# The first expert set's loop for leftover blocks, moved from behind its last unit to ahead of it

## The chip, the cores and the metric

The kernel runs on one core of a Trainium2 chip. It is one launch; the metric is its device time in microseconds. The core's engines each work through an instruction list of their own: TensorE (PE, with its weight loads as PEld), VectorE (DVE), ScalarE (ACT), GpSimd (POOL) and SyncE (SP), which here mainly issues the DMA transfers from HBM.

## The reference

Two transformer blocks follow one another on 512 tokens of width 1024, in fp32. Each ends with a mixture of experts. In the first, a token goes to 2 of 32 experts:

```python
hid = jax.nn.silu(a) * u * gates[:, sl, None].astype(hf.dtype)
out = out + jnp.einsum('nef,efd->nd', hid, w_d[sl]).astype(jnp.float32)
```

`a` and `u` are a token's products with an expert's gate and up matrix (1024 to 256), `w_d` leads back from 256 to 1024. The second block begins with `h = rms_norm(x, g_mix_norm) * (1.0 + scale_m) + shift_m` on the sum of all this, and projects `h` with `w_in` (`proj = h @ w_in`). Its own mixture has 64 experts, 6 for a token.

## The kernel before

The stages stand in the order of the program: `phase_a` (attention of the first block), `phase_b` (its experts), `phase_c` (mixer of the second block), `phase_d` (its experts). Here it is the end of `phase_b` and the start of `phase_c`.

**Units.** The tokens of an expert fill slots of 32, 64 or 128 rows; a unit is 128 rows from two or three experts, which were ranked by their number of tokens. The first set has 13 units (0 to 12), the second 33; unit 12 has three experts (64, 32 and 32 rows). For a unit SP loads three matrices of 1 MB for each expert: `wg`, `wu`, `wd` (`load`, line 802), so nine for unit 12, up to three units ahead (`fetch`). `main` makes on PE the product `g` with `wg` and `u` with `wu` (line 973), on ACT and DVE `hid` from both (lines 975 and 979), on PE the transposed `hT` (984), then the product `y` with `wd` (997), which ACT and DVE split into a high and a low part, `yh` and `yl`. The scatter (`scatter`, lines 1051 and 1052) multiplies these with the 0/1 matrix `st` on PE into banks `sc`, and DVE adds each to the residual `xres`. The scatter of a unit is made within the next unit's `main`, between `u` and `y`, most of it ahead of `hT`; that of unit 12 comes at the end of `run`. PE's and DVE's order inside `main` is that of the code; all else is ordered by a scheduler.

**The loop for leftover blocks.** Tokens that find no slot go through `spill`: a loop (line 1144) with a count that is known only at run time. Each turn loads one expert and treats 128 rows of it. Where a loop begins, all engines meet, SP also with the transfers of its queue; the loop's body is left out if the count is zero. In `phase_b` it stands behind everything else:

```python
moe.run()
early[1](moe.gathered.ins)
...
early[2](junk)
moe.spill(lambda: early[2](junk))
```

Here `early[1]` has POOL make the row `gs` of the next norm.

**What comes next.** `early[2]` is `stats` (line 1472): for each of four blocks of 128 tokens ACT sums the squares (into a waste tile `junk`), and `rsqrt` (lines 87 to 97) makes the factor `rs`. `phase_c` then makes `h` from `xres`, `rs` and `gs` on DVE (line 1511, eight halves), PE transposes it (`xt`, 1514), ACT and DVE split it into `xh` and `xl` (1518, 1519), and the projection `pr` (lines 108 to 110) multiplies both with the high and low parts `wh` and `wl` of `w_in` (`weights`: load 130, ACT 136, POOL 137). Two pieces of `w_in` have room at a time. The load of `mw` (line 1398) is for later sums.

Of the kernel before, what the change touches and what calls it, by code (L numbers as in the profile page):

```python
# [7 lines left out]
F32 = mybir.dt.float32  # L8
F32R = mybir.dt.float32r
# [11 lines left out]
KD = 8  # L21
# [724 lines left out]
class Moe:  # L746
# [182 lines left out]
        c = FIRST[self.E] + u  # L929
        self.xs[u] = self.slots(self.sel.pop(u), self.k.cols[:, c:c + 1], None, self.xg[u % 2])  # L930

    def turn(self, xg):
        k, nc, m = self.k, self.k.nc, self.m
        xT = m.tile([128, KD, 128], F32, tag="xT", name="xT", bufs=1)
        for h in range(2):
            b = k.bank("xT")
            for j in range(4):
                nc.tensor.transpose(b[:, j * 128:(j + 1) * 128], xg[:, 4 * h + j::8], k.ident)  # L938
            nc.scalar.activation(xT[:, 4 * h:4 * h + 4], b.rearrange("p (k s) -> p k s", k=4), AF.Copy)
        return xT  # L940
# [64 lines left out]
            self.k.nc.vector.tensor_mul(y, b, self.scale[:, h * 512:(h + 1) * 512])  # L1005
        return y

    def parts(self, out):

        k, m = self.k, self.m  # L1010

        def put(h, b):
            yh = m.tile([128, 512], F32R, tag="yh", name="yh", bufs=2)
            yl = m.tile([128, 512], F32R, tag="yl", name="yl", bufs=2)
            out.append((yh, yl))
            k.split(yh, yl, self.scaled(h, b, b))
        return put
# [34 lines left out]
                nc.vector.tensor_add(self.acc[:, t, hs], self.acc[:, t, hs], b)  # L1052
                yield

    def run(self):
        n = len(self.units)
        for u in range(2):
            self.pick(u)
        self.prep(0)
        with self.k.tc.issue_after(self.indexed.ins):  # L1060
            self.prep(1)
        if self.E == 32:
            self.fetch(3, after=self.gathered.ins, free=NF)
        self.take(0)
        self.pick(2)
        self.prep(2)
        self.table()
        self.pick(3)
        for u in range(n):
            self.fetch(u + FA)  # L1070
            with self.k.tc.manual_schedule(engines={self.k.nc.tensor.engine, self.k.nc.vector.engine}):
                self.main(u)
        for _ in self.scatter(*self.sofar.pop()):
            pass
# [64 lines left out]
    def spill(self, then=None):  # L1139

        k, nc, tc, m, E = self.k, self.k.nc, self.k.tc, self.m, self.E
        tbl = self.tbl
        n = nc.values_load(self.nb[0:1, 0:1], min_val=0, max_val=NB - 1)
        with tc.For_i(0, n, 1) as i:
            row = m.tile([128, 4], F32, name="row")
            nc.sync.dma_start(row, tbl[bass.ds(i, 1), :].to_broadcast([128, 4]))
            ei = m.tile([1, 1], I32, name="ei")
            nc.vector.tensor_copy(ei, row[:1, 3:4])
            ev = nc.sync.value_load(ei[0:1, 0:1], min_val=0, max_val=E - 1)
            ws = [(128, self.load([ev])[0])]  # L1150
            sel = m.tile([128, 128], F32R, name="selx")
            nc.vector.tensor_scalar(sel, row[:, 2:3].to_broadcast([128, 128]), k.cols[:, 0:1], None, op0=ALU.is_equal)
            xg = self.xg[0]
            st = self.slots(sel, k.cols[:, 2:3], row[:, 0:1], xg)
            gc = m.tile([128, 1], F32, name="gcx")
            jk = m.tile([128, E], F32, name="jkx")
            nc.vector.scalar_tensor_tensor(jk, k.tok[:, :E], row[:, 1:2], xg[1], op0=ALU.is_equal, op1=ALU.mult,
                                           accum_out=gc)
            y = []
            self.ffn(self.turn(xg[0]), ws, gc, self.parts(y))  # L1160
            for _ in self.scatter(st, y):
                pass
            if then is not None:
                then()
# [48 lines left out]
def top1(k, pool, v, n, name):  # L1213

    nc = k.nc
    shp = list(v.shape)
    mx = pool.tile(shp[:-1], F32, name=name + "m")
    oh = pool.tile(shp, F32, name=name + "o")
    nc.vector.tensor_reduce(mx, v, axis=AX.X, op=ALU.max)
    bc = lambda a: a.unsqueeze(len(shp) - 1).to_broadcast(shp)  # L1220
    nc.vector.tensor_tensor(oh, v, bc(mx), op=ALU.is_equal)
    rv = k.rev[:, None, 64 - n:].to_broadcast(shp)
    nc.vector.tensor_mul(oh, oh, rv)
    fm = pool.tile(shp[:-1], F32, name=name + "f")
    nc.vector.tensor_reduce(fm, oh, axis=AX.X, op=ALU.max)
    nc.vector.tensor_tensor(oh, rv, bc(fm), op=ALU.is_equal)
    return oh, mx


def phase_b(k, early):  # L1230
# [3 lines left out]
    def order():  # L1234
        while True:
            yield from OB
# [4 lines left out]
    moe = Moe(k, 32, I["w_exp_gate"][0], I["w_exp_up"][0], I["w_exp_down"][0], None, ctx, UNITS1, RB, order(), expert=expert)  # L1241
# [11 lines left out]
    gc = p.tile([128, KD], F32, name="gc")  # L1253
# [7 lines left out]
    def turn(t):  # L1261
        for q in range(2):
            b = k.bank("xt")
            for j in range(4):
                c = (4 * q + j) * 128
                nc.tensor.transpose(b[:, j * 128:(j + 1) * 128], k.xres[:, t, c:c + 128], k.ident)
            nc.scalar.activation(xTs[:, t % 2, 4 * q:4 * q + 4], b.rearrange("p (k s) -> p k s", k=4), AF.Copy)

    def logits(t):
        for kk in range(KD):  # L1270
            nc.tensor.matmul(lbs[0][:, t * 36:(t + 1) * 36], lhsT=xTs[:, t % 2, kk], rhs=wr[:, kk], start=kk == 0,
                             stop=kk == KD - 1)
# [23 lines left out]
    def rest():  # L1296
        moe.rooms()
        moe.work()
        early[0](k.wloads[-1])
        moe.fetch(2, 0, spread=[None] * NW + [written[i] for i in WS])  # L1300
        turn(NT - 1)
        logits(NT - 2)
        logits(NT - 1)
        moe.acc, lb = k.xres, lbs[0]
        v = Carve(moe, (("yh", 2), ("yl", 2)))
        L = v.tile([128, NT, 36], F32, name="L")
        for t in range(NT):
            nc.vector.scalar_tensor_tensor(L[:, t], lb[:, t * 36:(t + 1) * 36], rss[t], br, op0=ALU.mult, op1=ALU.add)
        go, gm = top1(k, v, L[:, :, :4], 4, "g")
        es = v.tile([128, NT, 4, 8], F32, name="es")  # L1310
        nc.vector.tensor_mul(es, L[:, :, 4:].rearrange("p t (g e) -> p t g e", g=4),
                             go[:, :, :, None].to_broadcast([128, NT, 4, 8]))
        sel = v.tile([128, NT, 8], F32, name="selv")
        nc.vector.tensor_reduce(sel, es.rearrange("p t g e -> p t e g"), axis=AX.X, op=ALU.add)
        o1, m1 = top1(k, v, sel, 8, "e")
        nc.vector.scalar_tensor_tensor(sel, o1, NEG, sel, op0=ALU.mult, op1=ALU.add)
        o2, m2 = top1(k, v, sel, 8, "f")
        on = v.tile([128, NT, 8], F32, name="on")
        nc.vector.tensor_add(on, o1, o2)

        def spread_(eng, dst, src):
            eng.tensor_mul(dst.rearrange("p t (g e) -> p t g e", g=4), src[:, :, None, :].to_broadcast([128, NT, 4, 8]),
                           go[:, :, :, None].to_broadcast([128, NT, 4, 8]))
        A = p.tile([128, NT, 32], BF, name="A")
        spread_(nc.vector, A, on)

        po = nc.gpsimd
        eg = v.tile([128, NT, 4], F32, name="eg")
        po.tensor_sub(eg, L[:, :, :4], gm[:, :, None].to_broadcast([128, NT, 4]))
        nc.scalar.activation(eg, eg, AF.Exp)  # L1330
        po.tensor_sub(m2, m2, m1)
        nc.scalar.activation(m2, m2, AF.Exp)
        gs = v.tile([128, NT], F32, name="gs")
        with tc.high_priority(-HP):
            nc.vector.tensor_reduce(gs, eg, axis=AX.X, op=ALU.add)
            nc.vector.scalar_tensor_tensor(gs, m2, 1.0, gs, op0=ALU.add, op1=ALU.mult)
            nc.vector.reciprocal(gs, gs)
        po.tensor_mul(m2, m2, gs)
        b8 = lambda a: a[:, :, None].to_broadcast([128, NT, 8])
        po.tensor_mul(o1, o1, b8(gs))  # L1340
        po.tensor_mul(o2, o2, b8(m2))
        po.tensor_add(o1, o1, o2)
        G = v.tile([128, NT, 32], F32, name="G")
        spread_(po, G, o1)
        moe.positions(A, v, perm)
        moe.ranked(G, v, p)
        moe.run()
        early[1](moe.gathered.ins)
        junk = moe.slot([128, 2, D], F32, "junk")
        k.root(moe.silu)  # L1350
        early[2](junk)
        moe.spill(lambda: early[2](junk))
        ctx.close()
        k.wr_ctx.close()
    return head, rest
# [696 lines left out]
```

## Time and profile before

| | us |
|---|---|
| three runs: lowest, median, highest | 1668.68, 1671.65, 1672.71 |
| the profiled execution, its own time | 1676.92 |
| its span | 1675.2 |
| PE busy in the span | 1550.9 (93%) |
| unit 12's `g` starts | 597.05 |
| last scatter of the first set ends on PE | 621.20 |
| first loads of `phase_c` leave SP | 627.66 |

The span is cut from the first to the last instruction on the chip; all starts below are from its begin. A timeline row gives start, length, engine, line, operation and in brackets the engine's idle time ahead of it and what ended it. Rows of a queue (SPq) are issues. A row with a count is merged from so many instructions.

### The profile page before, as it was taken

Reading aid. Unit: us, or ns where it says so; the run is one execution under the profiler, and the core shown is the slowest. Engines: PE = TensorE matmul, PEld = TensorE weight load, DVE = VectorE, ACT = ScalarE, POOL = GpSimd, SP = SyncE. Lnnn points to the kernel's source line nnn. Section 1 sums busy time; section 2 is a strip of 40 time slices with the busy share of each in tenths; the row PEclk is TensorE's granted clock in tenths of the full one; section 3 lists DMA queues with packets and bytes.
Section 4 is the critical chain, followed back from the end, with each engine's and each line's share of the span. In section 5 each row is a group of like instructions: output and inputs, shape, how many; then the busy total and the mean of one; then the engine's idle time right before and its main releaser. Section 6 shows DMA issues by size and latency. Waiting matters only on the chain.

```text
span 1675.2 us, 28638 instructions
## 1 busy us (share of the span) xinstructions
PE 1550.9 (93%) x10917; PEld 1060.7 (63%) x10917; DVE 970.1 (58%) x2219; ACT 542.3 (32%) x1090; POOL 347.4 (21%) x287
## 2 busy tenths in 40 slices
PE   5899999978998877899999998999999999999996
PEld 5665557765565546675667777865666666666663
DVE  3598536853564348547455534555665665656656
ACT  4534676331211125555553322301211211112112
POOL 2323551012111103330104441131111101111000
PEclk9999999987999998999999999899999999999998
DMA  5443336468999953233006837748899999999961
GB/s 187 147 162 114 107 82 233 132 214 321 418 416 417 419 239 105 72 104 90 26 5 203 255 104 276 285 168 366 366 411 386 396 412 415 418 414 422 419 259 64
DMA packets 104207, 420.78 MB, mean 251 GB/s; under 512 B 23444, under 2 KB 30074, under 8 KB 66692
## 3 DMA queue, kind: packets, MB, share of 16 engines
q1 hardware_dynamic: 82880, 389.25, 60.5%
q0 software_dynamic: 9968, 19.04, 3.1%
q10 hardware_dynamic: 11220, 10.63, 2.0%
q8 instruction: 87, 1.43, 0.3%
q14 instruction: 52, 0.43, 0.1%
HBM read 419.99 MB, written 9.21 MB: 256 GB/s over the span
## 4 chain that ended last, share of the span: by engine, by line
PE 46%; DVE 5%; DMA 4%; POOL 1%; ACT 1%; issue 1%; SPq 0%; DVEq 0%; ACTq 0%; POOLq 0%
PE g L973 8%; PE u L973 8%; PE sc L1051 7%; PE y L997 7%; PE qk L1671 2%; DMA mw<-in_w_mod_dram 2%; PE ob L1699 2%; PE xT L938 2%; PE pt L110 1%; PE pt L109 1%; PE pt L108 1%; PE pt L1691 1%; DVE macc L1400 1%; POOL wl L137 1%; DMA gmr<-in_g_ffn_norm_dram 1%
## 5 line engine op out<-in xcount | busy, mean ns | idle before, releaser
L137 POOL TENSOR_TENSOR wl<-w,wh 128x1024 fp32r<-128x1024 f32 (+4 forms) x72 | 166.7, 2316 | 366.4 <-ACT wh L136 343.9
L1052 DVE TENSOR_TENSOR xres<-xres,sc 128x512 f32<-128x512 f32 x368 | 224.5, 683 | 4.2 <-PE sc L1051 1.0
L973 PE MATMUL u<-wu,xT 128*32 128x256 f32 (+2 forms) x2240 | 180.4, 388 | 12.3 <-DMA wu<-in_w_exp_up_dram 10.0
L973 PE MATMUL g<-wg,xT 128*32 128x256 f32 (+2 forms) x2240 | 177.9, 383 | 1.1 <-DMA wg<-in_w_exp_gate_dram 1.1
L915 POOL DMA_INDIRECT xg<-hD,ii x46 | 46.1, 1001 | 609.4 <-issue 504.3
L997 PE MATMUL y<-wd,hT 128*32 128x512 f32 (+2 forms) x1120 | 167.6, 596 | 0.0
L973 PEld LDWEIGHTS u<-wu,xT 128*32 128x32 f32 (+2 forms) x2240 | 120.8, 121 | 61.5 <-DMA wu<-in_w_exp_up_dram 12.4
L979 DVE SCALAR_TENSOR_TENSOR hid<-u,gc,hid 128x256 f32<-128x256 f32 x46 | 22.3, 484 | 236.4 <-PE u L973 236.4
L973 PEld LDWEIGHTS g<-wg,xT 128*32 128x32 f32 (+2 forms) x2240 | 103.8, 119 | 86.4 <-issue 33.7
L1051 PE MATMUL sc<-yh,st 128*128 128x512 f32 x368 | 152.2, 416 | 0.0
L136 ACT ACTIVATE wh<-w 128x1024 fp32r<-128x1024 f32 (+4 forms) x88 | 89.9, 1021 | 184.2 <-PE pt L109 81.6
L1051 PE MATMUL sc<-yl,st 128*128 128x512 f32 x368 | 144.4, 395 | 0.1
L987 ACT ACTIVATE hT<-hT 128x256 f32<-128x256 f32 x46 | 17.7, 384 | 299.7 <-PE hT L984 299.7
L116 ACT ACTIVATE yh<-y 128x512 fp32r<-128x512 f32 x92 | 54.9, 597 | 162.8 <-DVE y L1005 104.7
L108 PE MATMUL pr<-wh,xh 128*128 128x512 f32 (+2 forms) x256 | 102.1, 403 | 5.7 <-ACT wh L136 5.2
L109 PE MATMUL pr<-wl,xh 128*128 128x512 f32 (+2 forms) x256 | 101.4, 398 | 6.1 <-POOL wl L137 6.1
L997 PEld LDWEIGHTS y<-wd,hT 128*32 128x32 f32 (+2 forms) x1120 | 46.6, 118 | 90.7 <-issue 88.5
L117 DVE TENSOR_TENSOR yl<-y,yh 128x512 fp32r<-128x512 f32 x92 | 63.6, 691 | 67.1 <-ACT yh L116 55.5
L110 PE MATMUL pr<-wh,xl 128*128 128x512 f32 (+2 forms) x256 | 100.6, 397 | 0.2 <-DVE xl L117 0.2
L110 PE MATMUL pt<-xh,wl 128*128 128x512 f32 x224 | 89.4, 399 | 3.0 <-POOL wl L137 3.0
L108 PE MATMUL pt<-xh,wh 128*128 128x512 f32 x224 | 90.3, 403 | 0.3 <-DVE qM L1620 0.2
L109 PE MATMUL pt<-xl,wh 128*128 128x512 f32 x224 | 89.0, 398 | 0.0
(535 smaller groups left out, 2819.2 us busy)
## 6 DMA issues: line engine op xcount, KB each, us to landing
wg<-in_w_exp_gate_dram SPq DMA_DIRECT2D x96, 1024.0 KB
wu<-in_w_exp_up_dram SPq DMA_DIRECT2D x96, 1024.0 KB
wd<-in_w_exp_down_dram SPq DMA_DIRECT2D x96, 1024.0 KB
w<-in_w_in_dram SPq DMA_DIRECT2D x52, 512.0 KB
mw<-in_w_mod_dram SPq DMA_DIRECT2D x32, 512.0 KB
mw<-in_w_mod_dram SPq DMA_DIRECT2D x8, 1024.0 KB
w<-in_w_out_dram SPq DMA_DIRECT2D x16, 512.0 KB
brs<-brd ACTq DMA_DIRECT2D x1, 2560.0 KB
```

Of the source, the lines that this page charges most:

```text
L108: nc.tensor.matmul(out, lhsT=lh, rhs=rh, start=first, stop=False)
L109: nc.tensor.matmul(out, lhsT=lh, rhs=rl, start=False, stop=False)
L110: nc.tensor.matmul(out, lhsT=ll, rhs=rh, start=False, stop=last)
L116: hi = nc.scalar.activation(dh, src, AF.Copy)
L117: lo = nc.vector.tensor_sub(dl, src, dh.bitcast(F32))
L136: nc.scalar.activation(wh[:, :, :c], w[:, :, :c], AF.Copy)
L137: (eng or nc.gpsimd).tensor_sub(wl[:, :, :c], w[:, :, :c], wh[:, :, :c].bitcast(F32))
L915: self.gathered = nc.gpsimd.indirect_dma_start(out=x, out_offset=None, in_=src, in_offset=bass.IndirectOffsetOnAxis(ap=ii[:, :1], axis=0), ...
L973: nc.tensor.matmul(b[sl], lhsT=xT[:, kk, sl], rhs=g[h][:, kk], start=kk == 0, stop=kk == KD - 1)
L997: nc.tensor.matmul(b[sl], lhsT=hT[:, j, sl], rhs=d[:, j, h * 512:(h + 1) * 512], start=j == 0, stop=j == 1)
L1051: nc.tensor.matmul(b, lhsT=st[:, ts], rhs=y[h][i], start=i == 0, stop=i == 1)
L1052: nc.vector.tensor_add(self.acc[:, t, hs], self.acc[:, t, hs], b)
```

## The change

`run` gets a function `early`. Ahead of the last unit (u = n - 1) it now makes the scatter of the unit before, then calls `early` (POOL's row `gs`) and `spill`; only then follows `main` of the last unit. The call of `spill` at the end of `phase_b`, with the repeat of the norm's sums in it, is gone. The loop's body now takes its `xT`, `yh` and `yl` from two slots of the weight pools (`xTx`, `yx`). The second set calls `run` without `early`, so its loop stays at the end, with the same new slots.

```diff
--- before.py
+++ after.py
...
-    def turn(self, xg):
+    def turn(self, xg, xT=None):
         k, nc, m = self.k, self.k.nc, self.m
-        xT = m.tile([128, KD, 128], F32, tag="xT", name="xT", bufs=1)
+        if xT is None:
+            xT = m.tile([128, KD, 128], F32, tag="xT", name="xT", bufs=1)
...
-    def parts(self, out):
+    def parts(self, out, room=None):
...
-            yh = m.tile([128, 512], F32R, tag="yh", name="yh", bufs=2)
-            yl = m.tile([128, 512], F32R, tag="yl", name="yl", bufs=2)
+            if room is None:
+                yh = m.tile([128, 512], F32R, tag="yh", name="yh", bufs=2)
+                yl = m.tile([128, 512], F32R, tag="yl", name="yl", bufs=2)
+            else:
+                yh, yl = room[:, 2 * h], room[:, 2 * h + 1]
...
-    def run(self):
+    def run(self, early=None):
...
         for u in range(n):
             self.fetch(u + FA)
+            if u == n - 1 and early:
+
+                for _ in self.scatter(*self.sofar.pop()):
+                    pass
+                early()
+                self.spill()
             with self.k.tc.manual_schedule(engines={self.k.nc.tensor.engine, self.k.nc.vector.engine}):
                 self.main(u)
         for _ in self.scatter(*self.sofar.pop()):
...
-            self.ffn(self.turn(xg[0]), ws, gc, self.parts(y))
+            xT = self.slot([128, 2, KD, 128], F32, "xTx")[:, 0]
+            self.ffn(self.turn(xg[0], xT), ws, gc, self.parts(y, self.slot([128, 4, 512], F32R, "yx")))
...
-        moe.run()
-        early[1](moe.gathered.ins)
+        moe.run(lambda: early[1](moe.gathered.ins))
         junk = moe.slot([128, 2, D], F32, "junk")
         k.root(moe.silu)
         early[2](junk)
-        moe.spill(lambda: early[2](junk))
         ctx.close()
```

Lines of the changed kernel are some 9 to 10 higher: 1144 is now 1154, 973 is 974, 997 is 998, 1051 is 1055, 1511 is 1520.

**SP around the loop**, before. A wait on DMAHW0 to DMAHW7 is one on a transfer that went through SP's or ACT's queue (they take turns); the branch waits for all of these and then for the other engines (a second, longer row, left out).

```order
L802 DMA wd<-in_w_exp_down_dram 128x2048 [waits DMAHW2_49,PE_49]
L802 ISA
L802 DMA wd<-in_w_exp_down_dram 128x2048 [waits DMAHW3_49,PE_49]
L1143 TENSOR_LOAD nb [waits DVE_49]
L1143 ISA x2
L1398 DMA mw<-in_w_mod_dram 128x1024 [waits DMAHW4_49,Pool_49]
L1144 COMPARE_AND_BRANCH
L1144 UNCONDITIONAL_BRANCH [waits SP_sequencer_49,DMAHW0_49,DMAHW5_49,DMAHW6_49,DMAHW7_49]
```

The last of the nine loads of unit 12, then the count, `mw` and the branch. The same place in the change:

```order
L802 DMA wd<-in_w_exp_down_dram 128x2048 [waits DMAHW2_49,PE_49]
L802 ISA
L802 DMA wd<-in_w_exp_down_dram 128x2048 [waits DMAHW3_49,PE_49]
L1153 TENSOR_LOAD nb [waits DVE_49]
L1154 COMPARE_AND_BRANCH
L1154 UNCONDITIONAL_BRANCH [waits SP_sequencer_49,DMAHW4_49,DMAHW5_49,DMAHW6_49,DMAHW7_49]
```

All nine loads of unit 12 stand ahead of the loop in both; only `mw` has moved behind it, and the loop of the change is followed by `mw` and the loads of `w_in`.

**PE at unit 12**, before: all of `g` and the first rows of `u`. The scatter of unit 11, `hT` and `y` follow, and the loop only behind unit 12's own scatter.

```order
L973 MATMUL g<-wg,xT 32x256 [waits DMAHW3_49,DVE_49,Activation_49]
L973 MATMUL g<-wg,xT 32x256
L973 MATMUL g<-wg,xT 32x256 [waits DMAHW4_49]
L973 MATMUL g<-wg,xT 32x256 [waits DMAHW5_49]
L973 MATMUL g<-wg,xT 32x256 x12
L973 MATMUL g<-wg,xT 32x256 [waits Activation_49]
L973 MATMUL g<-wg,xT 32x256 x15
L973 MATMUL u<-wu,xT 32x256 [waits DMAHW6_49,DVE_49]
L973 MATMUL u<-wu,xT 32x256
L973 MATMUL u<-wu,xT 32x256 [waits DMAHW7_49]
L973 MATMUL u<-wu,xT 32x256 [waits DMAHW0_49]
```

Each of the three matrices of `wg` and of `wu` is guarded by a wait for its own transfer, and `y` waits in the same way for each `wd`. The change, from the end of the loop on:

```order
L974 MATMUL g<-wg,xT 32x256 x32
L974 MATMUL u<-wu,xT 32x256 x32
L985 MATMUL hT<-ident,hid 128x128 [waits DVE_49]
L985 MATMUL hT<-ident,hid 128x128
L998 MATMUL y<-wd,hT 32x512 [waits Activation_49]
L998 MATMUL y<-wd,hT 32x512 x15
L1055 MATMUL sc<-yh,st 128x512 [waits Activation_49]
L1055 MATMUL sc<-yl,st 128x512 [waits DVE_49]
```

Unit 12 now lies behind the loop, without a wait for a transfer and without unit 11's scatter in its middle.

**DVE between the last scatter and `h`**, before, from the last two factors to the branch into the loop:

```order
L89 RECIPROCAL rs1r<-rs1y 128x1 [waits Activation_49]
L95 TENSOR_SCALAR rs1y<-rs1y 128x1 [waits DVE_49]
L91 SCALAR_TENSOR_TENSOR rs1y<-rs1r,rs1u 128x1 [waits DVE_49]
L97 TENSOR_TENSOR rs_2779<-rs1r,rs1y 128x1 [waits DVE_49]
L95 TENSOR_SCALAR rs1y<-rs1y 128x1 [waits DVE_49]
L97 TENSOR_TENSOR rs_2779<-rs1r,rs1y 128x1 [waits DVE_49]
L1143 TENSOR_LOAD nb [waits DVE_49]
L1144 COMPARE_AND_BRANCH
L1144 UNCONDITIONAL_BRANCH [waits DVE_49]
```

The four `h` follow only behind the loop. In the change, the same steps are:

```order
L97 TENSOR_TENSOR rs_2779<-rs1r,rs1y 128x1 [waits DVE_49]
L91 SCALAR_TENSOR_TENSOR rs1y<-rs1r,rs1u 128x1 [waits DVE_49]
L97 TENSOR_TENSOR rs_2779<-rs1r,rs1y 128x1 [waits DVE_49]
L89 RECIPROCAL rs1r<-rs1y 128x1 [waits Activation_49]
L95 TENSOR_SCALAR rs1y<-rs1y 128x1 [waits DVE_49]
L1520 SCALAR_TENSOR_TENSOR h<-xres,rs_2779,gs 128x512
L97 TENSOR_TENSOR rs_2779<-rs1r,rs1y 128x1 [waits DVE_49]
L91 SCALAR_TENSOR_TENSOR rs1y<-rs1r,rs1u 128x1
L1520 SCALAR_TENSOR_TENSOR h<-xres,rs_2779,gs 128x512
L95 TENSOR_SCALAR rs1y<-rs1y 128x1 [waits DVE_49]
L1520 SCALAR_TENSOR_TENSOR h<-xres,rs_2779,gs 128x512
L97 TENSOR_TENSOR rs_2779<-rs1r,rs1y 128x1 [waits DVE_49]
```

`h` now follows the first factors directly, mixed with the steps of the others. On ACT the first split of `w_in` (line 136) now stands between the sums and the four roots.

## Rows read from the trace of the kernel before

**Rows 1.** The page's first line.
```profile
span 1675.2 us, 28638 instructions
```

**Rows 2.** The page's costliest groups: the gated product `hid`, all units.
```profile
L979 DVE SCALAR_TENSOR_TENSOR hid<-u,gc,hid 128x256 f32<-128x256 f32 x46 | 22.3, 484 | 236.4 <-PE u L973 236.4
```

**Rows 3.** Timeline of PE, DVE and ACT in unit 12.
```profile
597.05 0.61 PE L973 MATMUL g<-wg,xT 128*32 128x256 f32 x6
598.46 3.42 PE L973 MATMUL g<-wg,xT 128*32 128x256 f32 x57 [0.80 <-DMA wg<-in_w_exp_gate_dram]
...
603.43 0.62 PE L973 MATMUL u<-wu,xT 128*32 128x256 f32 x2 [1.31 <-DMA wu<-in_w_exp_up_dram]
605.90 3.64 PE L973 MATMUL u<-wu,xT 128*32 128x256 f32 x58 [1.86 <-SPq L1144]
...
609.64 0.48 DVE L979 SCALAR_TENSOR_TENSOR hid<-u,gc,hid 128x256 f32<-128x256 f32 x1 [11.02 <-PE u L973]
...
612.87 0.38 ACT L987 ACTIVATE hT<-hT 128x256 f32<-128x256 f32 x1 [8.83 <-PE hT L984]
...
613.63 3.64 PE L997 MATMUL y<-wd,hT 128*32 128x512 f32 x32
...
620.80 0.40 PE L1051 MATMUL sc<-yl,st 128*128 128x512 f32 x1
```

**Rows 4.** The loop's line in short windows: queue, count, ns (min/median/max), first to last start.
```profile
L1144 SPq COMPARE_BRANCH  x1: 53/53/53, 596.5 to 596.5; - x1
...
L1144 SPq EVENT_SEMAPHORE  x2: 28/28/28, 608.4 to 610.9; - x2
...
L1144 SPq EVENT_SEMAPHORE  x1: 13767/13767/13767, 613.3 to 613.3; - x1
...
L1144 PEldq COMPARE_BRANCH  x1: 179/179/179, 627.8 to 627.8; - x1
...
L1144 DVEq COMPARE_BRANCH  x3: 41/51/61, 627.2 to 628.8; - x3
```

**Rows 5.** Stretches of 2 us: busy of each engine, PEclk, DMA share, GB/s.
```profile
604.00:606.00 2.00, 0.14 (x5) 0.10 (x8) 0.00 (x0) 0.04 (x1) 0.00 (x0) 1.00 0.94 389
612.00:614.00 2.00, 2.00 (x13) 1.25 (x15) 2.00 (x5) 0.38 (x1) 0.00 (x0) 1.00 0.23 92
624.00:626.00 2.00, 0.00 (x0) 0.00 (x0) 1.13 (x13) 1.26 (x6) 0.00 (x0) 0.52 0.00 0
634.00:636.00 2.00, 0.82 (x3) 0.50 (x3) 2.00 (x5) 2.00 (x7) 2.00 (x2) 0.92 0.01 4
```

**Rows 6.** Timeline from the last scatter into the projection, row by row of several engines.
```profile
625.61 0.15 DVE L97 TENSOR_TENSOR rs<-rs1r,rs1y 128x1 f32<-128x1 f32 x1
...
627.66 4.49 SPq L130 DMA_DIRECT2D w<-in_w_in_dram  x4
...
629.03 2.74 DVE L1511 SCALAR_TENSOR_TENSOR h<-xres,rs,gs 128x512 f32<-128x512 f32 x4 [2.35 <-POOL f L1602]
...
629.84 3.68 PE L1514 MATMUL xt<-ident,h 128*128 128x128 f32 x16 [8.64 <-DVE h L1511]
...
631.00 0.37 ACT L1518 ACTIVATE xh<-xt,shc 128x128 fp32r<-128x128 f32 x1 [5.74 <-DMA w<-in_w_in_dram]
...
632.36 0.91 ACT L136 ACTIVATE wh<-w 128x848 fp32r<-128x848 f32 x1
...
633.35 4.80 POOL L137 TENSOR_TENSOR wl<-w,wh 128x848 fp32r<-128x848 f32 x2 [5.05 <-DMA w<-in_w_in_dram]
...
634.83 1.45 DVE L1511 SCALAR_TENSOR_TENSOR h<-xres,rs,gs 128x512 f32<-128x512 f32 x1
...
635.77 0.46 PE L109 MATMUL pr<-wl,xh 128*128 128x424 f32 x1 [1.13 <-POOL wl L137]
```

**Rows 7.** Timeline of PE in the first set's first unit, on either side of the clock's rise.
```profile
391.85 3.67 PE L973 MATMUL g<-wg,xT 128*64 128x256 f32 x14
...
397.65 2.54 PE L973 MATMUL u<-wu,xT 128*64 128x256 f32 x21
```

## The prediction, before the changed kernel was run

> **What bounds the kernel now.** I read the page first, for the span and for whether the loop for leftover blocks ever runs. The span is 1675.2 us [rows 1]. The gated product `hid` was made 46 times [rows 2], which is once for each of the 13 units of the first set and the 33 of the second. So neither loop did a single turn, and all that either costs is its entry and its exit, where the engines meet. What matters is therefore only what is in flight when they meet.
>
> Next the timeline of PE around the first set's last unit (unit 12). It starts at 597.05 and waits for its weights: the first product for `wg` until 598.46, the second for `wu` until 603.43 and 605.90. Then PE makes the scatter of unit 11, from 613.63 for 3.64 us unit 12's third product, then its scatter, and is done at 621.20 (620.80 plus 0.40) [rows 3]. I call that end T.
>
> Then the queue of SP. It is at the loop already at 596.5, since all its weight loads are issued by then, and there it waits for transfers: events at 608.4, 610.9 and 613.3 [rows 4]. With PE's two waits for `wu` at 603.43 and 605.90 [rows 3] these make one series with a step of 2.4 to 2.5 us, one for each transfer of a matrix: the last two `wu`, then the three `wd`. So the last `wd` lands at 613.3. The 13.767 us after it are SP waiting for the other engines [rows 4]. The DMA engines' rate falls from 389 to 92 GB/s meanwhile [rows 5]: some of the 16 finish early, and the slowest set each landing.
>
> Last the stretch from T to the next stage. The stage's first weight loads leave SP at 627.66, behind the loop, and ACT can split them at 632.36. DVE has the first normalising factor at 625.61 (and 0.15), but begins with `h` only at 629.03, behind the loop. PE transposes from 629.84 for 3.68 us and runs the projection steadily from 635.77, when POOL's `wl` is there [rows 6]. From T to there 14.6 us pass, of which PE works 4 to 5.
>
> **The change, part by part.** *The loop moves ahead of unit 12.* On SP nothing moves but one load of `mw`: it stood ahead of the loop and now stands behind it. The nine loads of unit 12 stay ahead. SP's branch into the loop waits for every queue it has used, and behind the loop unit 12's products carry no wait for a transfer any more, where each matrix had one before. So the meeting holds PE until the last `wd` has landed, at 613.3. The transfers were issued by the turn of their own queue, not by anything that PE does later, so I leave 613.3 as it is. The way out of the meeting: the last to arrive was DVE at 627.2, and PE's last step there was at 627.8 and took 0.18, so 0.8 us; DVE itself needed until 628.8 [rows 4]. PE restarts at 613.3 + 0.8 = 614.1, with DVE's way out as the upper bound, 614.9. Before, PE was in unit 12 from 597 on.
>
> *Unit 12 then runs whole, with nothing beside it.* 57 of the first product's matmuls took 3.42 us and 58 of the second's 3.64 [rows 3]; 64 of each make 3.84 + 4.02 = 7.9 us.
>
> Its scatter of unit 11 has been pulled ahead of the loop, where it costs nothing: it takes 3.9 us, as that of unit 12 did (617.27 to 621.20), and PE has 17 us between 597 and 614. But it was the cover for the step from the second product to the third, which is now bare: the product ends at 609.54, `hid` starts 0.10 later and takes 0.48, the third product starts 0.76 after ACT's `hT` at 612.87 [rows 3], and between them lie two transposes with their handovers, some 0.7 (my estimate: two such steps like the 0.10, and about as much work as ACT's 0.38 on the same tile): 2.0 us. Third product and scatter as before: 613.63 to 621.20, 7.6 us.
>
> *The clock.* PE will have stood idle for some 13 us. In the old gap, empty from 621.2, the granted clock was 0.52 in 624 to 626; PE resumed at 629.84 and the 0.92 of 634 to 636 puts the return near 634.3, so 4.5 us after [rows 5, 6]. At the lower level (1.2 GHz) 14 matmuls of this product took 3.67 us, at the upper (2.4 GHz) 21 took 2.54 [rows 7], 2.17 times as long for one. 4.5 us at that rate lose 4.5 x (1 - 1/2.17) = 2.4 us. Bounds: nothing, and 4.
>
> The new T is 614.1 + 7.9 + 2.4 + 2.0 + 7.6 = 634.0, against 621.2: 12.8 us later.
>
> *Behind T no engine meets any other.* SP sends the new stage's loads at about 614, and by the old distance (627.66 to 632.36, 4.7 us, and one `mw` ahead) they are in by 620. ACT splits the first of them right behind the squares and POOL makes `wl`; POOL's two took 4.8 us [rows 6] and stand behind a memset that now waits for PE, so even if that is PE's last scatter they end at T + 5.4. The norm: first factor at T + 4.4 as before, 0.9 more because ACT now splits a weight ahead of the four roots, and half a microsecond of the other rows' steps; `h` starts at T + 5.8, not T + 7.8 (629.03). Sixteen transposes stand ahead of the first projection in either order; they ended at T + 12.3 (633.52) and now end at T + 10.3. With the weights there the projection runs from T + 10.3, not T + 14.6: 4.3 us back. I take 4.0, since DVE, which makes an `h` in 0.7 and an `xl` for each step of the projection, must now keep up. Lower bound 2.0, if PE waits for `xl` and only the norm's two remain; upper 6.4, if the projection starts on the first split `xh` (631.00 and 0.37, less 2.0: T + 8.2).
>
> One more thing lies in that bound. While POOL made the two `wl`, one of DVE's `h` took 1.45 us, where four took 2.74 together [rows 6]; the two `wl` now lie ahead of `h`. The Trainium skill's page "SBUF — State Buffer", section "Who interferes with whom", says that a VectorE instruction with two inputs in SBUF and a GpSimd one that reads SBUF exclude one another for a whole instruction. By it up to 0.7 us more would come back; the row bears it out once, and I leave it to the bound.
>
> **The sum.** 12.8 - 4.0 = +8.8 us. On the profiled execution's own 1676.92 us that is 1685.7. The median of the three runs is 1671.65, 5.3 us under the profiled one, and what is moved here is the same in both: 1671.65 + 8.8 = 1680.5 us. The known bounds are 12.8 - 2.4 - 6.4 = +4.0 and 12.8 + 0.8 + 1.6 - 2.0 = +13.2.
>
> **The rivals.** (a) *The exit gives back more.* If the projection starts on the first `xh` and PE gets its clock back at once, the lower bounds of both terms hold: +4.0, 1675.7 us, no difference that can be measured. For it: PE works 4 to 5 us in 14.6, so there is room. Against it: the chain square, root, `h`, transpose, `xh` has no slack and stays, and the old gap shows the clock's delay.
>
> (b) *The meeting holds no weights.* If the branch waited only for the engines, unit 12 would start when unit 11's scatter is added up: PE ends it at 601, and DVE's rest and the way out take more than 0.8 and less than the 6.8 from T to PE's way out, which had the norm in it; I take 3, so 604. The products end at 612 with `wu` there since 605.9, the third starts at 614 with `wd` in since 613.3, and T is 621.6, 0.4 later. With 4.0 back the change gives -3.6, 1668.1 us, not slower. It turns on one point: whether PE's first product of unit 12 may start before 613.3; below about 609 the exit's gain wins. For it: SP, not PE, issues the transfers. Against it: the three events on SP, and the absence of any other wait that would guard these products.
>
> (c) *The exit gives nothing back.* If DVE, which has both `h` and `xl` to make, or the third pair of weights becomes the limit, all of the 12.8 remains: 1684.5 us. For it: PE had a store of `xl` to begin with at 635.77, which it will lack. Against: the loads are 20 us earlier against T than they were.
>
> That the change does not do what it says is excluded by the order of the instructions. A loop that did turn would be another matter, but 46 excludes it.
>
> **How the numbers follow.** Forecast 0.62, (a) 0.17, (b) 0.06, (c) 0.15. A measurement of this kernel tells a difference from none at about 0.3%, 5.0 us. Slower by more than that: the forecast, (c), and a small part of (a) that ends just above, 0.79. Within: most of (a) and of (b), 0.17. Faster: what of (b) comes with the full 6.4, 0.04. The predicted time is 1680.5. The range runs from 1674.5 to 1686 (+2.9 to +14.4): the lower end takes in (a), the upper (c) with the bounds of clock and way out. Left out are (b) and the tails.
>
> **What would show it.** In the new profile PE should fall silent near 601 and start unit 12 at 614 at a granted clock of 0.5; its products should have no wait for `wg`, `wu` or `wd`; T should lie near 634, with the step from second to third product of 2 us bare. SP should issue `w_in` near 614; `h` should start 6 us after T and the projection run from 10. The prediction is wrong if PE restarts before 610, or if the projection runs within 7 us of T.

## The result, and the profile after

| | before | changed |
|---|---|---|
| median of seven runs each, us | 1671.64 | 1683.88 |
| ratio to the kernel before, with its 95% interval | | 1.0063, 1.0045 to 1.0081 |
| the profiled execution's own time, us | 1676.92 | 1688.46 |
| its span, us | 1675.2 | 1686.6 |

The change makes the kernel slower: by the ratio 10.5 us (7.5 to 13.5), by the medians 12.2. The forecast was 1680.5, +8.8; rival (c), in which the exit gives nothing back, stood at 1684.5.

Two stretches carry the account from here on. The first runs from the start of unit 11's third product `y` to T, the end of the last scatter. The second runs from T to the end of the first projection's last product (`pr` of 424 columns). The rows of before that [rows 3, 6] do not hold are these two starts (timeline of PE: start, length, engine, line, operation):

```profile
593.59 3.64 PE L997 MATMUL y<-wd,hT 128*32 128x512 f32 x32
...
655.68 0.35 PE L110 MATMUL pr<-wh,xl 128*128 128x424 f32 x1
```

With T at 621.20 the first stretch took 27.6 us before, the second 34.8 (655.68 + 0.35 - 621.20). The same timeline of the changed kernel:

```profile
593.48 3.64 PE L998 MATMUL y<-wd,hT 128*32 128x512 f32 x32
...
600.66 0.40 PE L1055 MATMUL sc<-yl,st 128*128 128x512 f32 x1
615.58 6.07 PE L974 MATMUL g<-wg,xT 128*32 128x256 f32 x64 [14.52 <-DMA wd<-in_w_exp_down_dram]
621.40 3.70 PE L974 MATMUL u<-wu,xT 128*32 128x256 f32 x64
...
626.73 3.64 PE L998 MATMUL y<-wd,hT 128*32 128x512 f32 x32 [0.47 <-ACT hT L988]
...
633.90 0.40 PE L1055 MATMUL sc<-yl,st 128*128 128x512 f32 x1
...
644.03 3.69 PE L1523 MATMUL xt<-ident,h 128*128 128x128 f32 x16 [9.73 <-DVE h L1520]
...
647.37 0.58 PE L108 MATMUL pr<-wh,xh 128*128 128x424 f32 x1
...
668.90 0.36 PE L110 MATMUL pr<-wh,xl 128*128 128x424 f32 x1
```

T is 634.30 (633.90 + 0.40). The first stretch is 40.8 us, 13.2 longer; the second is 35.0, as long as before. PE falls silent behind unit 11's scatter at 601.1 and does nothing for 14.5 us, and what ended that is a load of `wd`, which the first product does not even read. The queue of SP at the loop's line (count, ns, first and last start) says the same as [rows 4]:

```profile
L1154 SPq COMPARE_BRANCH  x1: 53/53/53, 595.7 to 595.7; - x1
...
L1154 SPq EVENT_SEMAPHORE  x1: 28/28/28, 609.7 to 609.7; - x1
...
L1154 SPq EVENT_SEMAPHORE  x1: 28/28/28, 612.2 to 612.2; - x1
...
L1154 SPq EVENT_SEMAPHORE  x2: 28/28/28, 614.7 to 614.8; - x2
```

The three `wd` land 2.5 us apart, the last at 614.7, and PE is at work 0.9 us later. In stretches of 2 us (busy time of PE, PEld, DVE, ACT, POOL with instructions in brackets, then the granted clock, the DMA share and GB/s):

```profile
604.00:606.00 2.00, 0.00 (x0) 0.00 (x0) 0.00 (x0) 0.00 (x0) 0.00 (x0) 0.50 0.96 397
...
616.00:618.00 2.00, 2.00 (x24) 1.62 (x20) 0.00 (x0) 0.00 (x0) 0.00 (x0) 0.50 0.72 168
...
620.00:622.00 2.00, 2.00 (x40) 1.73 (x36) 0.00 (x0) 0.31 (x1) 0.00 (x0) 0.91 0.54 173
...
646.00:648.00 2.00, 2.00 (x12) 1.98 (x11) 2.00 (x7) 1.50 (x5) 0.00 (x0) 0.58 0.00 0
```

No engine works while the transfers run out, and unit 12's first product then runs at the lower clock. The second stretch is decided by a few rows of POOL and DVE between T and `h`:

```profile
638.82 3.90 POOL L137 TENSOR_TENSOR wl<-w,wh 128x848 fp32r<-128x848 f32 x2 [3.94 <-ACT wh L136]
638.86 0.26 DVE L89 RECIPROCAL rs1r<-rs1y 128x1 f32<-128x1 f32 x2 [0.74 <-ACT rs1y L88]
639.06 3.67 DVE L91 SCALAR_TENSOR_TENSOR rs1y<-rs1r,rs1u 128x1 f32<-128x1 f32 x2
...
643.24 0.74 DVE L1520 SCALAR_TENSOR_TENSOR h<-xres,rs,gs 128x512 f32<-128x512 f32 x1
```

Two instructions of DVE on a single column, each with two inputs in SBUF, take 3.67 us. They end when POOL's two `wl` end, and `h` starts 8.9 us behind T, where the forecast had 5.8. The two reciprocals, which have one input, take no longer beside the same `wl` (0.26 for both) than two of them did before, with nothing on POOL (0.26).

### The profile page after: what moved, and what is told of

Read it like the earlier page. It is cut to its first block, busy times and chain, and to the rows that moved or that the text cites. A ratio compares the mean times of both kernels' runs of the same rounds, so it can differ in the third digit from the quotient of the medians.

```text
span 1686.6 us, 28627 instructions
## 1 busy us (share of the span) xinstructions
PE 1547.6 (92%) x10917; PEld 1045.9 (62%) x10917; DVE 973.3 (58%) x2219; ACT 543.1 (32%) x1090; POOL 345.1 (20%) x287
## 4 chain that ended last, share of the span: by engine, by line
PE 47%; DVE 4%; DMA 3%; POOL 1%; ACT 1%; issue 1%; SPq 0%; DVEq 0%; ACTq 0%; POOLq 0%
PE g L974 7%; PE u L974 7%; PE sc L1055 7%; PE y L998 7%; PE qk L1680 2%; PE ob L1708 2%; PE pt L110 2%; PE pt L108 2%; PE pt L109 2%; PE xT L939 2%; DMA mw<-in_w_mod_dram 1%; PE pt L1700 1%; DVE macc L1409 1%; DMA w<-in_w_in_dram 1%; POOL wl L137 1%; DMA gmr<-in_g_ffn_norm_dram 1%
## 5 line engine op out<-in xcount | busy, mean ns | idle before, releaser
L974 PE MATMUL g<-wg,xT 128*32 128x256 f32 (+2 forms) x2240 | 174.8, 387 | 15.6 <-DMA wd<-in_w_exp_down_dram 14.5
L974 PE MATMUL u<-wu,xT 128*32 128x256 f32 (+2 forms) x2240 | 172.1, 382 | 7.4 <-DMA wu<-in_w_exp_up_dram 7.4
L974 PEld LDWEIGHTS u<-wu,xT 128*32 128x32 f32 (+2 forms) x2240 | 104.5, 119 | 66.3 <-DMA wu<-in_w_exp_up_dram 9.5
## 6 DMA issues: line engine op xcount, KB each, us to landing
wg<-in_w_exp_gate_dram SPq DMA_DIRECT2D x96, 1024.0 KB, 14.6
wu<-in_w_exp_up_dram SPq DMA_DIRECT2D x96, 1024.0 KB, 12.2
```

The costliest lines, as they stand in the source:

```text
L974: nc.tensor.matmul(b[sl], lhsT=xT[:, kk, sl], rhs=g[h][:, kk], start=kk == 0, stop=kk == KD - 1)
```

## The experiments

Stretches are from one profiled execution of each kernel, in us; the ratio is to the kernel before.

| kernel | first | second | ratio, 95% interval |
|---|---|---|---|
| before | 27.6 | 34.8 | |
| changed | 40.8 | 35.0 | 1.0063, 1.0045 to 1.0081 |
| e1, changed without the loop | 29.7 | 35.0 | 0.9985, 0.9968 to 1.0002 |
| e2, before without the loop | 27.4 | 36.2 | 1.0004, 0.9987 to 1.0020 |
| e3, `wd` behind the loop | 32.0 | 35.8 | 1.0027, 1.0009 to 1.0044 |
| e4, low parts first | 41.2 | 36.5 | 1.0068, 1.0045 to 1.0090 |
| e5, and positions held | 38.5 | 32.2 | 1.0033, 1.0017 to 1.0048 |
| e6, `wl` behind the factors | 40.7 | 32.4 | 1.0059, 1.0032 to 1.0085 |
| e7, PE kept at work | 42.8 | 43.4 | 1.0103, 1.0079 to 1.0126 |
| e8, loop ahead of the last scatter | 31.4 | 34.2 | 1.0013, 0.9995 to 1.0030 |
| e9, e3 and e5 together | 31.9 | 35.1 | 1.0002, 0.9984 to 1.0021 |
| e10, e2 and e5 together | 32.0 | 31.6 | 0.9971, 0.9951 to 0.9990 |

What lies behind the second stretch took between 1013.5 and 1019.2 us in these twelve executions, 1019.2 in the profile of before and 1017.3 in that of the change. So the stretches tell where time goes, and their sum agrees with the ratio only to some us.

**e1 and e2: without the loop.** From the changed kernel, then from the one before:

```diff
-                self.spill()
```
```diff
-        moe.spill(lambda: early[2](junk))
```

> The changed kernel with the first set's loop taken out (for this data it makes no turn, so nothing that is computed is lost); the scatter of unit 11 still stands ahead of unit 12. Theory (the meeting holds PE for weights in flight): PE starts unit 12 at about 601 instead of 615.6, its products end before the last wd, which in the changed kernel's trace lands at 614.7, and the last scatter ends near 622.5 instead of 634.3, so 11.8 us less. Behind it the split of the next weights meets h and not the small factors, 0 to 3 us less. Together 12 to 15 us under the changed kernel, near 1670. Rival (PE would have been late at this place without a meeting too, for instance because the products are slow after the pulled-out scatter): the last scatter ends after 628, and less than 6 us are gained.

> The kernel before with the first set's loop taken out (it makes no turn). Theory (the meeting behind the last scatter costs what its exit holds back): the last scatter still ends near 621, since nothing met there before, and the next stage's weights are there long before it; the steady projection starts 10 to 12 us after the scatter instead of 14.6, so 3 to 4 us less than before, 1668. Rival (what follows the scatter is bound by squares, roots, h and transposes alone): within 1 us of before.

Without the meeting the first stretch is 29.7 us, 11.1 less than in the changed kernel, and in time its loss is gone (0.9985). So neither the pulled-out scatter nor the order around unit 12 costs much; the meeting does. The gain at the exit, however, is not there in either kernel. In e2 the first `h` transposes begin 4.6 us behind T (before: 8.6), and still the projection ends no earlier. Its timeline and stretches:

```profile
627.86 3.68 PE L1513 MATMUL xt<-ident,h 128*128 128x128 f32 x16 [4.61 <-DVE rs1y L95]
...
632.01 1.08 PE L108 MATMUL pr<-wh,xh 128*128 128x424 f32 x2 [0.47 <-ACT wh L136]
632.04 4.43 POOL L137 TENSOR_TENSOR wl<-w,wh 128x848 fp32r<-128x848 f32 x2 [8.21 <-ACT wh L136]
```
```profile
632.00:634.00 2.00, 1.08 (x2) 0.50 (x2) 1.70 (x6) 2.00 (x7) 1.96 (x1) 0.50 0.00 0
...
638.00:640.00 2.00, 2.00 (x9) 1.93 (x8) 0.59 (x3) 0.99 (x4) 0.00 (x0) 0.50 0.73 207
640.00:642.00 2.00, 2.00 (x13) 1.83 (x12) 0.92 (x5) 0.94 (x4) 0.00 (x0) 0.84 0.00 0
```

The weights are in SBUF long before, but ACT splits them only behind the first `xh`, POOL follows, PE stops in between, and its clock stays at 0.50 until about 640, 17 us behind T (before: 13, [rows 5]). The rival of e2 came out: within 1 us of before, though not because squares, roots, `h` and transposes were the limit.

**e3: what the meeting waits for.**

```diff
+            if self.E == 32 and self.loaded == len(self.units) - 1:
+                self.late.append((g[i][2], sl(self.wd, e)))
+                continue
             self.last.append(get(g[i][2], sl(self.wd, e)))
...
                 self.spill()
+                for dst, src in self.late:
+                    self.k.nc.sync.dma_start(dst, src)
```

> The changed kernel, but the three wd of unit 12 are loaded behind the loop instead of ahead of it. Theory (the meeting waits for the transfers in flight): the last wu lands at 607.2, PE restarts at about 608.1 instead of 615.6, the two products take 9.5, the three wd land by about 618 beside them, the last scatter ends near 627, and the kernel is 7 to 8 us faster than the changed one, near 1676. Rival (the meeting takes its time whatever is in flight): PE restarts at 615 or later, and with the loads behind it the kernel is as slow as the changed one or slower, 1684 and more.

PE restarts 13.5 us behind the start of unit 11's `y` (592.17) instead of 22.1, and the first stretch loses 8.8 us:

```profile
605.70 5.44 PE L978 MATMUL g<-wg,xT 128*32 128x256 f32 x64 [5.96 <-issue]
...
623.78 0.39 PE L1059 MATMUL sc<-yl,st 128*128 128x512 f32 x1
```

The ratio falls from 1.0063 to 1.0027, some 6 us. The meeting costs what is still in flight, and three loads less are three landings of 2.5 us less. This is the clearest of the verdicts.

**e4 and e5: the low parts ahead of the squares.** In e4 the first two pieces of `w_in` are split first, and the norm's squares follow behind ACT's splits; e5 adds the second edit.

```diff
+    first = [k.weights(pw, [(w_in, 0, 416), (w_in, 1952, 1960)], 2 * i, 2, 512, 2) for i in range(2)]
+    hi, lo = k.made
+    with tc.issue_after(hi.ins):
...
+    with tc.issue_after(lo.ins):
```
```diff
-    nc.vector.tensor_copy(pf, pi)
+    with tc.issue_after(k.rooted.ins):
+        nc.vector.tensor_copy(pf, pi)
```

> The changed kernel, but in the next stage the high and low parts of the first two pieces of w_in (ACT's wh, POOL's wl) are made ahead of the norm's squares instead of between squares and roots; the memset that stood ahead of wl on POOL stands behind it. Theory (POOL's wl held DVE's small factors for 3.5 us): those two instructions on DVE take 0.4 us again instead of 3.67, h starts about 5 us after the last scatter instead of 8.9, and the projection runs steadily from 9.8 after it instead of 13.1: 3 to 4 us less than the changed kernel, near 1680. Rival (DVE waited there for ACT's roots or for the half clock's PE): the factors are as late as in the changed kernel, and the time stays within 1 us of it.

> The kernel of the run before this (high and low parts of the first two pieces of w_in ahead of the squares), and in addition DVE's work on the positions, which there slipped in front of the norm's factors, is held behind the last factor. Theory (once nothing of POOL's lies beside the factors and nothing of DVE's in front of them, the exit gives back what the forecast said): h starts at about 5 us behind the last scatter instead of 8.9, the projection ends 31 to 32 us behind it instead of 35.0, and the kernel is 3 to 4 us faster than the changed one, near 1680. Rival (the end of the projection is set by something else, such as the half clock or the third and fourth piece's weights): h starts that early, but the projection still ends 34 to 36 us behind the scatter and the time stays that of the changed kernel.

e4 missed. The factors' own steps are short again, but the scheduler put DVE's work on the positions ahead of them, and `h` starts 9.3 us behind T. Its first instruction there, a cast of four columns, stands beside POOL's second `wl` and the memset behind it (to 630.66) and takes 1.96 us:

```profile
628.74 1.96 DVE L1540 CAST pf<-pi 128x4 f32<-128x4 int32 x1
```

e5 takes that away. `h` starts 4.3 us behind T, the second stretch is 32.2, and the ratio falls to 1.0033, 5 us below the changed kernel. It also has 2.3 us less in its first stretch, which the edits do not touch; so about 2.8 of the 5 are the exit's.

**e6: POOL's `wl` behind the factors.** The same question from the other side:

```diff
+    k.soon = nc.gpsimd.tensor_copy(sm.tile([128, 1], F32, name="ss"), rs4[:, 3:4])
...
+                    hold.enter_context(self.tc.issue_after(self.soon.ins))
```

> The changed kernel, but POOL's first wl of the next stage waits for the last of the norm's four factors (a copy of one column on POOL stands between). Theory (POOL's wl holds DVE's small instructions for as long as it runs): the two instructions of 3.67 us take 0.35 again, h starts at about 5.8 us behind the last scatter instead of 8.9; wl now runs beside h and xl and stretches those, so the projection ends 33 to 35.5 behind it, 0 to 2 us less in time. Rival (those two instructions waited for something else): they take as long as in the changed kernel, and everything else is 2 us later.

```profile
633.74 0.35 DVE L93 SCALAR_TENSOR_TENSOR rs1y<-rs1r,rs1u 128x1 f32<-128x1 f32 x2
...
637.66 1.97 POOL L143 TENSOR_TENSOR wl<-w,wh 128x848 fp32r<-128x848 f32 x1
638.08 2.10 DVE L1526 SCALAR_TENSOR_TENSOR h<-xres,rs,gs 128x512 f32<-128x512 f32 x1
```

The two instructions of 3.67 us take 0.35, `h` starts 5.6 us behind T (the forecast's 5.8), and now an `h` that takes 0.74 elsewhere takes 2.10 beside `wl`. The second stretch is 32.4. In time e6 lies 0.7 us under the changed kernel by the ratios, with an interval of over 4 on either side, so its verdict rests on the trace.

**e7: PE kept at work in its gaps.**

```diff
                 early()
+                self.warm(75)
                 self.spill()
...
+        if early:
+            self.warm(55)
...
+                k.nc.tensor.matmul(b[:, :128], lhsT=k.ident, rhs=k.ident, start=True, stop=True)
```

> The changed kernel with PE kept at work in its two gaps: 75 products of the unit matrix with itself (128x128) ahead of the meeting and 55 behind the last scatter, whose result nobody reads. Theory (the half clock behind both gaps costs 1.6 us in unit 12's products and 2 or more in the transposes and the first projections): the granted clock stays at 1.00 up to the meeting and through the gap behind the scatter, the two products take 8 instead of 9.5, transposes 2.4 instead of 3.7, and the kernel is 2.5 to 4 us faster than the changed one, 1680 to 1681. Rival (PE is not what the exit waits for while its clock is low): the clock is up, but the projection ends as late as before, and 1 to 1.5 us are gained in unit 12 alone.

This missed by its size: a product of the unit matrix is two instructions, 75 of them took 16.91 us, and the meeting then waited for PE itself, which restarted 26.5 us behind unit 11's `y` instead of 22.1. The scheduler also put the positions' work ahead of the first `xh`, so the second stretch tells nothing. What stands is the price of the clock in unit 12:

```profile
596.34 16.91 PE L1094 MATMUL warm<-ident 128*128 128x128 f32 x150
615.39 3.66 PE L974 MATMUL g<-wg,xT 128*32 128x256 f32 x64 [2.14 <-issue]
618.87 3.64 PE L974 MATMUL u<-wu,xT 128*32 128x256 f32 x64
```

Both products take 7.12 us (615.39 to 622.51) at the upper level, 9.52 in the changed kernel (615.58 to 625.10): 2.4 us for the clock.

**e8: the loop behind all loads.** Between the last unit's product and its scatter:

```diff
-            if u == n - 1 and early:
...
                 self.main(u)
+        if early:
+            early()
+            self.spill()
         for _ in self.scatter(*self.sofar.pop()):
             pass
```

A second edit, left out here, puts a small root on ACT behind the loop, ahead of the norm's squares.

> The loop between the last unit's third product and its scatter, behind all weight loads of the set; unit 11's scatter is back inside unit 12. Theory (a meeting costs what it drains and what it holds back): nothing is in flight any more, so unit 12 starts and runs as in the kernel before; the meeting costs PE 1 to 3 us between product and scatter, the next loads leave some 4 us ahead of the scatter's end, and the exit is 0 to 2 us shorter than before: within 0.2% of the kernel before, 1669 to 1675. Rival (the move's loss was not in the weights in flight but in anything that a meeting inside the last unit brings): 6 us or more slower than before.

The first stretch is 31.4, 3.8 more than before: 2.2 us of idle at the meeting and a scatter at the lower clock (0.50 in 624 to 626). In the second, `wl` again holds the factors and `h`: a factor's last step took 1.93 us, an `h` 2.34.

```profile
631.26 2.34 DVE L1518 SCALAR_TENSOR_TENSOR h<-xres,rs,gs 128x512 f32<-128x512 f32 x1
...
633.52 1.93 DVE L97 TENSOR_TENSOR rs<-rs1r,rs1y 128x1 f32<-128x1 f32 x1
```

No place for the loop that was tried beats the one it had.

**e9 and e10: both edits at once.** e9 joins e3 and e5, e10 joins e2 and e5; both hold ACT's five small loads behind its high parts.

> The changed kernel with both of its losses taken away at once: the three wd of unit 12 loaded behind the loop, and in the next stage the high and low parts of the first two pieces made ahead of the squares, DVE's work on the positions behind the last factor, and ACT's five small loads behind its high parts. Theory (the loss is the weights that the meeting waits for plus POOL's hold on the factors): from the start of unit 11's third product to the last scatter 32 us as in the run with wd behind alone, from there to the projection's end 32 or a little less; together 64 against 62.4 in the kernel before, so 0 to 3 us over the kernel before, 1671 to 1675. Rival (the two do not add, since early loads of the next stage and late wd share the queue): the low parts come late, the second stretch is 34 to 36 as in the changed kernel, 1676 and more.

> The kernel before without the first set's loop (it makes no turn), with the same edits in the next stage: low parts first, positions behind the factors, ACT's small loads behind its high parts. Theory (without the meeting the exit was free to be shorter, and POOL's low parts and the half clock took it back): from the last scatter to the projection's end 29 to 32 us instead of 36.2 in the run without a loop and 34.8 before, and the time 3 to 6 us under the kernel before, 1666 to 1669. Rival (the exit is bound by the projection itself, whatever stands ahead of it): 34 us or more, within 1.5 us of the kernel before.

In time e9 is as fast as the kernel before (1.0002), as its theory said; in the trace its rival came out. The first stretch is 31.9, as in e3, but the second is 35.1, as in the changed kernel. SP sends the loads of `w_in` only at 620.54, after waiting 9.0 us for `wd` and 4.1 for PE; ACT splits them 1.0 us behind T (625.40), and the squares wait for that. So e9 does not show that the exit's loss was taken away together with the entry's. By the stretches it would be 4.6 us slower than before; this rest was not traced.

e10 is the fastest, 0.29% under the kernel before (0.10 to 0.49), some 5 us, as its theory said. Its second stretch is 31.6, 3.2 shorter than before, so its rival (34 or more) is out. Its first is 32.0, 4.4 longer: `wg` comes 1.5 us later behind the start of `y`, and the last 58 matmuls of `u` run at the lower clock (0.50 from 606 to 610, before 1.00) and take 6.55 us instead of 3.64 [rows 3]:

```profile
604.82 6.55 PE L973 MATMUL u<-wu,xT 128*32 128x256 f32 x58 [1.88 <-DMA wu<-in_w_exp_up_dram]
```

By the stretches of this one execution (1672.2 us, where the median of the seven runs is 1666.0) e10 would be 1.2 us slower than before. So the 3.2 us at the exit are shown; where the rest of the gain lies is not. And e10 has no loop, so it is not a version for tokens that do find no slot.

## Why the prediction came out as it did

**The entry was right.** The first stretch was forecast 12.8 us longer and is 13.2 longer; rival (b), in which PE starts unit 12 before 609, is out. Term by term: the last `wd` lands at 614.7, not 613.3, since in this execution the whole stream of loads ran 1.4 us later. PE restarts 0.9 behind it (forecast 0.8). Both products with the clock took 9.5 (forecast 7.9 + 2.4 = 10.3; the 2.4 was exact by e7, and the 7.9 was 0.8 too much). The bare step took 1.6 (2.0), product and scatter 7.6 (7.6). The mechanism held; that the sum fits to 0.4 us is in part luck, since 1.5 too little and 1.2 too much nearly cancel.

**The exit was wrong, and the step that failed is the start of `h`.** The forecast took it as T + 5.8 from three terms: the first factor as before, 0.9 for the weight that ACT splits ahead of the roots, half a microsecond for the other rows' steps. It is T + 8.9, since POOL's two `wl` run exactly there and hold DVE's steps for 3.3 us, a wait that the forecast put at nothing. By its own sum the two `wl` would have been nearly out of the way: it let them end at T + 5.4, counted from POOL's memset, though it also had ACT split the weight only behind the squares. POOL waited 3.94 us for that split, and the second `wl` ended at T + 8.4 (642.72).

PE then transposes from T + 9.7 (before: 8.6), has its weights at once and projects steadily from T + 13.1 (647.37; before: T + 14.6). That is 1.5 us back instead of 4.3, and these are used up ahead of the end: from there the projection takes 21.9 us, before 20.3. Before, two of its products stood ahead of that start, and PE then waited nowhere; now it waits 0.8 us in the middle for the low part of the third piece:

```profile
633.33 1.32 PE L108 MATMUL pr<-wh,xh 128*128 128x424 f32 x2
```
```profile
659.90 0.46 PE L109 MATMUL pr<-wl,xh 128*128 128x424 f32 x1 [0.79 <-POOL wl L137]
```

So 4.0 became nothing. The slack that the forecast named, DVE making `h` and `xl`, was not what counted. Rival (c) gave the right size. Of the two limits that it named, DVE was the larger, but through small instructions that no one had counted as work; the third pair of weights had the 0.8 us.

**A rule was at hand and was applied to the wrong rows.** The prediction drew on the Trainium skill, "SBUF — State Buffer", section "Who interferes with whom", for `h` beside `wl` alone, and so read it as a further gain. The rule asks what an instruction reads, not how long it is. By it a factor step with two inputs in SBUF that falls beside a `wl` lasts until that `wl` ends. Two such steps beside the two `wl`, 3.90 us long, lose some 3.5 us, an estimate, and the exit's gain would be 4.0 - 3.5 = 0.5 us. The trace agrees with the rule: 3.67 us for two instructions of 0.35, ended by POOL, and in e4 1.96 for a cast, which the same section lists among those that can take the shared ports. The prediction knew both halves, since it wrote that `wl` now lies ahead of `h`; what lies between T and `h` on DVE was the third.

**What the gain is without the hold.** e5 and e6 start `h` at T + 4.3 and T + 5.6, no later than the forecast had it, and the second stretch shrinks by 2.6 to 2.8 us, not 4.0. In both PE waits some 0.8 us for the third piece's `wl`, as in the changed kernel (0.85 at 655.86 in e5, 0.78 at 652.15 in e6). Whether the lower clock takes the rest was not tested by itself.

**The chances.** Slower by over 0.3% was given 0.79 and came true; 1683.88 lies inside 1674.5 to 1686. The size was nearer to (c), 1684.5, than to the forecast.

## What to carry to other kernels

Where all engines meet, count the bytes that the loading queue has in flight, not the instructions: here each load of 1 MB was 2.5 us of silence, on top of which PE paid 2.4 us for its clock. When work on POOL moves to another place, look at the instructions of DVE with two inputs in SBUF that it will stand beside, the smallest too, since each of them can last as long as POOL's. And a gain at an exit is real only when the next wait is named: here an earlier `h` met unsplit weights, and weights split early met the factors.

## What had not been expected of the hardware

An instruction of DVE on one column with two inputs, which takes 0.15 to 0.22 us alone, took up to 1.93 us beside a POOL instruction of 128x848. PE's clock stayed at 0.50 for some 13 us after PE had resumed in e2 (627.86 to about 640.6), where work came with pauses, against 3 to 4 us in the changed kernel (644.03 to about 647.7). And one product of two 128x128 matrices in fp32 appears as two instructions and takes 0.23 us.
